# Retention in a two-layer trunk: queries transposed two heads at a time into the keys' PSUM bank, decayed halves made by four VectorE multiplies

## The chip, the cores and the metric

The kernel runs on one core of one Trainium2 chip. A core has five engines that run side by side, each through its own list of instructions in a fixed order: TensorE (PE, with its weight loads shown apart as PEld), VectorE (DVE), ScalarE (ACT), GpSimd (POOL) and SyncE (SP), which here issues the DMAs. They wait for each other on semaphores. The metric is device time in microseconds (us); lower is better.

## The reference, cut to what matters

The program is one inference step of a trunk of two layers with 1280 tokens (256 of new context and 1024 latent ones, which also read a cache of 512). Each layer makes an input projection, feeds three token mixers from it (retention, grouped-query attention, latent attention), multiplies their outputs by a gate and projects back. The change lies in retention alone, which works on chunks of 128 tokens, four heads of 64 channels:

```python
def step(s, inp):
    qi, ki, vi = inp
    a = jnp.einsum('bihd,bjhd->bhij', qi, ki) * intra
    o = (jnp.einsum('bhij,bjhe->bihe', a, vi)
         + jnp.einsum('bihd,bhde->bihe', qi, s) * q_dec[None, :, :, None])
    s = s * c_dec[None, :, None, None] + jnp.einsum('bjhd,bjhe->bhde', ki * k_dec[None, :, :, None], vi)
    return s, o
```

It is run forward and backward over the tokens, and the two outputs are added and normalized. The kernel does both directions at once: a head's 64 query channels stand twice on the 128 partitions, in the upper half times the forward decay and in the lower half times the backward one, against a state that is stacked in the same way.

## The kernel before

A layer begins with projections. The last of these is the gate (`z_blk`, L671 to L693): long runs of matmuls at L683, L684 and L685 (128x512 or 128x256 results, called z below), each result followed by a tanh on ACT (L688), a multiply on DVE (L690) and a store by SP (L691). After every block `z_blk` pulls once at a generator, `aside` (L709), which hands out the layer's other work piece by piece: rotated keys, latents, retention, and then the first tiles of attention (`att.prepare`). So retention's small matmuls stand between z's, and z covers the waits of retention. A list scheduler in the framework then fixes the final order on every engine; the code's order is only its input.

Retention (L788 to L933) has a backward loop over the ten chunks that accumulates states (L834 and the lines at L821 to L845) and then a forward loop of 13 rounds in which four stages of different chunks overlap: `stage_c` of chunk t-2, `stage_b` of t-1, `stage_a` of t and `stage_d` of t-3.

- `stage_a`: POOL has copied the chunk's queries into a doubled tile `qq` (L399; every head's 64 columns twice). TensorE transposes it in four steps into a PSUM bank `pt` (L868) and the keys in two steps into a second bank `pk` (L871). DVE multiplies `pt` by the decays in one instruction of 128x512 (L875, gives `qdT`). ACT copies the queries from `pt` into the block-diagonal `BD` (L877, L878), which has one buffer, and the keys into `kT` (L880). The state for the next chunk is advanced on POOL (L825, L826).
- `stage_b`: two matmuls of keys and queries (L893), then the decay mask on DVE (L895, `At`).
- `stage_c`: eight small matmuls (L903, L904) into the bank of pool `o`, which has one bank; ACT squares them (L905), DVE sums (L907), runs a Newton iteration of 13 tiny instructions for the reciprocal root (L150 to L160) and scales (L910, `oret`). Since there is one such bank, L903 of the next chunk waits for L910.
- `stage_d`: two transposes of `oret` (L916) into the free half of `pk`, and a copy on ACT into `yx` (L917).

PSUM has eight banks: five for pool `acc` (z, and the results called m), two for `tp`, one for `o`. The tiles `kd`, `qq` and `At` share three buffers.

Behind retention the first tiles of attention come: SP loads pieces of the keys (L1086, L1090) and, in 16 issues a layer, the rotated latent keys (L1144); ACT casts them (L196, L1147); the first score matmuls are at L1247 and L1248, the softmax exponential on ACT at L1270, transposes of its result at L1288. The buffers of these tiles lie where retention's tiles were.

Of the kernel before, what the change touches and what calls it, by code (L numbers as in the profile page):

```python
# [10 lines left out]
F32 = mybir.dt.float32  # L11
# [3 lines left out]
ALU = mybir.AluOpType  # L15
# [3 lines left out]
P = 128  # L19
D = 1024  # L20
NL = 8
NT = 10
# [59 lines left out]
def hybrid_trunk(tc, I, O):  # L82
# [3 lines left out]
    V, A, G, T = nc.vector, nc.scalar, nc.gpsimd, nc.tensor  # L86
    dma = nc.sync.dma_start
    pin = tc.keep_in_program_order
# [23 lines left out]
    ident = cst.tile([P, P], F32, name="ident")  # L112
    dma(ident, I["ident"])
    yxs = cst.tile([P, NT, D], F32, name="yx")
    yx = [yxs[:, t, :] for t in range(NT)]
# [18 lines left out]
    def bank(tag):  # L134
        if tag == "o":
            return pp.tile([P, 512], F32, name=tag, tag=tag, bufs=1)
        if tag == "m":
            tag = "tp"
        bufs = {"acc": NACC, "tp": 7 - NACC}[tag]
        return pp.tile([P, 512], F32, name=tag, tag=tag, bufs=bufs)  # L140
# [257 lines left out]
    def pool_copy(o, i):  # L398
        return G.tensor_scalar(o, i, 1.0, 1.0, op0=ALU.mult, op1=ALU.mult)  # L399
# [388 lines left out]
    def retention(l, rt, load, kv):  # L788
# [12 lines left out]
        def h4(ap):  # L801
            return ap.rearrange("p (h d) -> p h d", h=4)

        F, B = slice(0, 64), slice(64, 128)
# [8 lines left out]
        decT = rt.tile([P, 4, 128], F32, name="decT")  # L813
# [4 lines left out]
        def advanced(eng, d, nxt, cur, inc=None):  # L818

            if inc is not None:  # L820
                eng.tensor_tensor(h4(nxt), h4(cur), bc(cdec[d], d.start, d.stop), op=ALU.mult)  # L821
                eng.tensor_tensor(nxt, nxt, inc, op=ALU.add)
            else:
                st = rt.tile([P, 256], F32, name="cur", tag="cur", bufs=2)[d]
                pin(eng.tensor_tensor(h4(st), h4(cur), bc(cdec[d], d.start, d.stop), op=ALU.mult))  # L825
                eng.tensor_tensor(nxt, nxt, st, op=ALU.add)  # L826

        def increments(t, kv):
            kd = rt.tile([P, 4, 2, 64], F32, name="kd", tag="kd", bufs=3)
            V.tensor_tensor(kd, h4(kv[:, 0:256]).unsqueeze(2).to_broadcast([P, 4, 2, 64]),  # L830
                            dec[:, 2:4, :].rearrange("p a h -> p h a").unsqueeze(3).to_broadcast([P, 4, 2, 64]), op=ALU.mult)
            ps = bank("m")
            for h in range(4):
                T.matmul(ps[:, h * 64:(h + 1) * 64], kd[:, h, :, :].rearrange("p a b -> p (a b)"),  # L834
                         kv[:, 256 + h * 64:256 + (h + 1) * 64], start=True, stop=True)

            if t not in (0, NL, NT - 1):
                advanced(V, B, S[B, t - 1, :], S[B, t, :], ps[B, :256])
            elif t == NL:
                advanced(V, B, fin[B, :], S[B, t, :], ps[B, :256])  # L840
            elif t == NT - 1:
                V.tensor_copy(S[B, t - 1, :], ps[B, :256])

            if t != NL - 1:
                A.copy(S[F, t + 1, :] if t != NT - 1 else fin[F, :], ps[F, :256])  # L845

        qqs = {}

        def doubled(t):
            if t < NT:  # L850
                qqs[t] = rt.tile([P, 4, 2, 64], F32, name="qq", tag="kd", bufs=3)
                pin(pool_copy(qqs[t], h4(yx[t][:, 0:256]).unsqueeze(2).to_broadcast([P, 4, 2, 64])))

        for t in range(NT - 1, -1, -1):
            yield
            nx_kv = load(t - 1) if t else load(0)
            increments(t, kv)
            if t < 2:
                doubled(1 - t)
            kv = nx_kv  # L860

        BD = rt.tile([P, 2, 256], F32, name="BD")
        V.memset(BD, 0.0)

        def stage_a(t, kv, qq):
            pt = bank("tp")
            for h in range(4):
                T.transpose(pt[:, h * 128:(h + 1) * 128], qq[:, h, :, :].rearrange("p a b -> p (a b)"), ident)  # L868
            pk = bank("tp")
            for j in range(2):  # L870
                T.transpose(pk[:, j * 128:(j + 1) * 128], kv[:, j * 128:(j + 1) * 128], ident)  # L871
            if t >= 3:
                stage_d(t - 3, outs.pop(t - 3), pk[:, 256:512])
            qdT = rt.tile([P, 4, 128], F32, name="qdT", tag="qdT", bufs=2)
            V.tensor_tensor(qdT.rearrange("p h c -> p (h c)"), pt, decT.rearrange("p h c -> p (h c)"), op=ALU.mult)  # L875
            pq = pt.rearrange("p (j x c) -> p x j c", j=2, x=2)
            A.copy(BD[0:64, :, 0:128], pq[0:64, 0])  # L877
            A.copy(BD[64:128, :, 128:256], pq[64:128, 1])  # L878
            kT = rt.tile([P, 2, 128], F32, name="kT", tag="kT", bufs=1)
            A.copy(kT.rearrange("p j c -> p (j c)"), pk[:, 0:256])  # L880

            if t < NL - 1:
                advanced(G, F, S[F, t + 1, :], S[F, t, :])
            elif t == NL:
                advanced(G, F, fin[F, :], S[F, NT - 1, :])
                for d in range(2):
                    dma(new_state[0, l, d].rearrange("h d e -> d h e"), h4(fin[64 * d:64 * d + 64, :]))
            return kv, qdT, kT

        def stage_b(kT):  # L890
            pa = bank("m")
            for j in range(2):
                T.matmul(pa[:, j * 256:(j + 1) * 256], kT[:, j, :], BD[:, j, :], start=True, stop=True)  # L893
            At = rt.tile([P, 4, 128], F32, name="At", tag="kd", bufs=3)
            V.tensor_tensor(At.rearrange("p h c -> p (h c)"), pa, MT.rearrange("p h c -> p (h c)"), op=ALU.mult)  # L895
            return At

        def stage_c(t, kv, qdT, At):
            bo = bank("o")
            po, sq = bo[:, 0:256], bo[:, 256:512]  # L900
            for h in range(4):
                hs = slice(h * 64, (h + 1) * 64)
                T.matmul(po[:, hs], At[:, h, :], kv[:, 256 + h * 64:256 + (h + 1) * 64], start=True, stop=False)  # L903
                T.matmul(po[:, hs], qdT[:, h, :], S[:, t, hs], start=False, stop=True)  # L904
            A.activation(sq, po, AF.Square)  # L905
            ss = sm.tile([P, 4], F32, name="ss4", tag="ss4")
            V.tensor_reduce(ss, h4(sq), axis=AX.X, op=ALU.add)  # L907
            rstd = newton(ss, 4, 1.0 / 64)
            o = rt.tile([P, 256], F32, name="oret", tag="cur", bufs=2)
            V.tensor_tensor(h4(o), h4(po), bc(rstd), op=ALU.mult)  # L910
            return o

        def stage_d(t, o, pt):

            for i in range(2):
                T.transpose(pt[:, i * 128:(i + 1) * 128], o[:, i * 128:(i + 1) * 128], ident)  # L916
            A.copy(yx[t][:, 0:256], pt)  # L917

        st, At, outs = {}, {}, {}
        for t in range(NT + 3):  # L920
            yield
            if 2 <= t < NT + 2:
                outs[t - 2] = stage_c(t - 2, st[t - 2][0], st[t - 2][1], At.pop(t - 2))
            if 1 <= t <= NT:
                At[t - 1] = stage_b(st[t - 1][2])
            if t < NT:
                nx_kv = load(t + 1) if t + 1 < NT else None
                if t:
                    doubled(t + 1)
                st[t] = stage_a(t, kv, qqs.pop(t))  # L930
                kv = nx_kv
            elif t >= 3:
                stage_d(t - 3, outs.pop(t - 3), bank("tp")[:, :256])  # L933

    def cache_keys(l, pool, bufs):
# [565 lines left out]
    def open_p1(ws):  # L1501
        st = ExitStack()
        p1 = st.enter_context(tc.tile_pool(name="p1", reuse_waits="tile", bufs=1))
        ws.p1 = p1
        acts = [[p1.tile([P, KC, m * 128], F32R, name=f"a{x}{b}") for x in "hl"] for b, m in BLOCKS]
        return st, p1, acts
# [11 lines left out]
    st, p1, acts = open_p1(ws)  # L1518
# [66 lines left out]
    for l in range(DEPTH):  # L1585
        ws = Weights(out_blocks(l) + (in_blocks(l + 1) if l + 1 < DEPTH else []))
        att.run(ws)
        st, p1, acts = open_p1(ws)
# [104 lines left out]
```

## Time and profile before

| | us |
|---|---|
| median of three runs | 2163.22 (2162.13 to 2165.70) |
| the profiled execution | 2162.85 |
| its span in the trace | 2161.1 |
| PE busy in the span | 2084.2 (96%) |
| DVE / ACT / POOL busy | 1502.0 / 1183.5 / 978.2 |

The span is what the trace covers; 1.75 us of the profiled execution lie around it. Times in rows are counted from the start of the span. An item such as "[1.18 <-DVE oret L910]" behind a row says that the engine stood idle for 1.18 us before this instruction, and that DVE's write of `oret` at L910 ended the wait. Layer 0's retention loop lies at about 411 to 488 us, layer 1's at about 1454 to 1529 us.

### The profile page before, as it was taken

Reading aid. Unit: us, or ns where it says so; the run is one execution under the profiler, and the core shown is the slowest. Engines: PE = TensorE matmul, PEld = TensorE weight load, DVE = VectorE, ACT = ScalarE, POOL = GpSimd, SP = SyncE. Lnnn points to the kernel's source line nnn. Section 1 sums busy time; section 2 is a strip of 40 time slices with the busy share of each in tenths; the row PEclk is TensorE's granted clock in tenths of the full one; section 3 lists DMA queues with packets and bytes.
Section 4 is the critical chain, followed back from the end, with each engine's and each line's share of the span. In section 5 each row is a group of like instructions: output and inputs, shape, how many; then the busy total and the mean of one; then the engine's idle time right before and its main releaser. Section 6 shows DMA issues by size and latency. Waiting matters only on the chain. (4 is left out here: it accounts for less than half of the span.)

```text
span 2161.1 us, 42292 instructions
## 1 busy us (share of the span) xinstructions
PE 2084.2 (96%) x14888; PEld 1870.0 (87%) x14888; DVE 1502.0 (70%) x3830; ACT 1183.5 (55%) x3180; POOL 978.2 (45%) x1444
## 2 busy tenths in 40 slices
PE   7999999999999999999999999998999999999998
PEld 3899987788888888888999999887788888888898
DVE  4625583666889999997174358546689899999824
ACT  3503333225788888886243233322488888888623
POOL 2341242315576465533543324233375656453474
PEclk8999999999999999999999999999999999999999
DMA  9542446414111010004143212452311111000322
GB/s 315 145 145 63 123 112 204 122 49 117 36 44 28 20 30 25 13 27 136 46 153 102 66 54 55 140 152 66 109 46 30 32 30 32 14 22 18 98 91 98
DMA packets 189117, 173.30 MB, mean 80 GB/s; under 512 B 35833, under 2 KB 171625, under 8 KB 188905
## 3 DMA queue, kind: packets, MB, share of 16 engines
q1 hardware_dynamic: 187464, 165.35, 25.7%
q10 hardware_dynamic: 1440, 5.24, 0.6%
q8 instruction: 119, 1.95, 0.4%
q14 instruction: 94, 0.76, 0.1%
HBM read 124.77 MB, written 45.76 MB: 79 GB/s over the span
## 5 line engine op out<-in xcount | busy, mean ns | idle before, releaser
L256 PE MATMUL acc<-wh,ah 128*128 128x256 f32 (+1 forms) x1760 | 503.4, 286 | 1.8 <-ACT ah L404 1.8
L258 PE MATMUL acc<-wh,al 128*128 128x256 f32 (+1 forms) x1760 | 500.6, 284 | 2.5 <-DVE al L405 2.4
L257 PE MATMUL acc<-wl,ah 128*128 128x256 f32 (+1 forms) x1760 | 502.7, 286 | 0.0
L1256 DVE TENSOR_REDUCE nm<-acc 128x1 f32<-128x512 f32 (+1 forms) x624 | 411.7, 665 | 39.0 <-PE acc L1250 27.0
L1293 DVE TENSOR_TENSOR pT<-tp,pT 128x512 fp32r<-128x512 f32 (+1 forms) x624 | 413.2, 664 | 36.1 <-ACT pT L1292 30.6
L1292 ACT CAST pT<-tp 128x512 fp32r<-128x512 f32 (+1 forms) x624 | 356.5, 573 | 139.1 <-PE tp L1288 132.8
L1270 ACT ACTIVATE pn<-acc,nm 128x512 f32<-128x512 f32 (+1 forms) x624 | 421.3, 681 | 19.9 <-DVE nm L1261 17.4
L1288 PE MATMUL tp<-ident,pn 128*128 128x128 f32 x2400 | 424.1, 274 | 3.9 <-DVE pT L1293 2.4
L256 PEld LDWEIGHTS acc<-wh,ah 128*128 128x128 f32 x1760 | 334.9, 190 | 13.1 <-issue 8.2
L258 PEld LDWEIGHTS acc<-wh,al 128*128 128x128 f32 x1760 | 332.0, 189 | 5.3 <-DVE al L405 4.5
L257 PEld LDWEIGHTS acc<-wl,ah 128*128 128x128 f32 x1760 | 334.0, 190 | 0.8 <-issue 0.8
L1304 PE MATMUL o<-pT,V 128*128 128x256 f32 x1200 | 326.3, 294 | 0.7 <-DVE yx L1317 0.6
L1288 PEld LDWEIGHTS tp<-ident,pn 128*128 128x128 f32 x2400 | 287.6, 140 | 34.6 <-PE tp L1288 5.8
L1305 PE MATMUL o<-pT,V 128*128 128x256 f32 x1200 | 314.4, 284 | 0.0
L1304 PEld LDWEIGHTS o<-pT,V 128*128 128x128 f32 x1200 | 227.1, 189 | 19.2 <-DVE yx L1317 5.1
L1305 PEld LDWEIGHTS o<-pT,V 128*128 128x128 f32 x1200 | 227.2, 189 | 16.6
L192 POOL TENSOR_SCALAR wh<-raw 128x512 fp32r<-128x512 f32 (+2 forms) x144 | 82.4, 582 | 321.2 <-PE acc L258 143.2
L193 POOL TENSOR_TENSOR wl<-raw,wh 128x512 fp32r<-128x512 f32 (+2 forms) x144 | 164.7, 1155 | 5.2
L1247 PE MATMUL acc<-K,Qm 128*128 128x512 f32 (+1 forms) x312 | 140.6, 451 | 1.0
L683 PE MATMUL acc<-ah,wh 128*128 128x512 f32 (+1 forms) x384 | 141.4, 368 | 0.0
L684 PE MATMUL acc<-ah,wl 128*128 128x512 f32 (+1 forms) x384 | 139.8, 364 | 0.0
L685 PE MATMUL acc<-al,wh 128*128 128x512 f32 (+1 forms) x384 | 139.5, 363 | 0.0
(278 smaller groups left out, 3898.3 us busy)
## 6 DMA issues: line engine op xcount, KB each, us to landing
raw<-in_w_ada_dram SPq DMA_DIRECT2D x96, 256.0 KB, 3.2
raw<-in_w_in_dram SPq DMA_DIRECT2D x56, 256.0 KB, 2.9
kv<-s_rkv SPq DMA_DIRECT2D x40, 256.0 KB, 2.8
s_gT<-eo SPq DMA_DIRECT2D x80, 128.0 KB, 2.2
yx<-in_x_sample_dram SPq DMA_DIRECT2D x16, 512.0 KB, 6.4
gt<-s_gT SPq DMA_DIRECT2D x60, 128.0 KB, 2.1
raw<-in_w_in_dram SPq DMA_DIRECT2D x56, 128.0 KB, 2.5
raw<-in_w_out_dram SPq DMA_DIRECT2D x48, 128.0 KB, 3.0
```

Source lines behind the costliest of these rows:

```text
L193: G.tensor_tensor(wl, raw, wh.bitcast(F32), op=ALU.subtract)
L256: T.matmul(ps, ah[:, k, :], wh, start=(k == 0), stop=False)
L257: T.matmul(ps, ah[:, k, :], wl, start=False, stop=False)
L258: T.matmul(ps, al[:, k, :], wh, start=False, stop=(k == KC - 1))
L683: T.matmul(ps, wh, ah[:, k, :], start=(k == 0), stop=False)
L1256: V.tensor_reduce(nm[:, b:b + 1], ps, axis=AX.X, op=ALU.max, negate=True)
L1270: A.activation(pn, ps, AF.Exp, bias=p.ng[i], accum_out=p.su[:, i, b:b + 1])
L1288: T.transpose(pt[:, c * 128:(c + 1) * 128], pn[:, c * 128:(c + 1) * 128], ident)
L1292: A.copy(ph, p3)
L1293: V.tensor_tensor(pl, p3, ph.bitcast(F32), op=ALU.subtract)
L1304: T.matmul(p.po, vc, p.gran[b][:, 0, c, :], start=(ch == 0), stop=False)
L1305: T.matmul(p.po, vc, p.gran[b][:, 1, c, :], start=False, stop=(ch == last))
```

## The change

Queries are no longer doubled. `stage_a` transposes the queries as they are, two heads at a time, in two steps into the left half of one bank, and the keys in two steps into its right half. ACT's two copies into `BD` and the copy `kT` come first in the code; then DVE makes the decayed queries in four multiplies of 64 partitions and 2x128 columns, one for each direction and each head of a pair, so that two of them write to the other half of the partitions than they read. `stage_d` gets a bank of pool `tp` of its own in every round.

```diff
-        def doubled(t):
-            if t < NT:
-                qqs[t] = rt.tile([P, 4, 2, 64], F32, name="qq", tag="kd", bufs=3)
-                pin(pool_copy(qqs[t], h4(yx[t][:, 0:256]).unsqueeze(2).to_broadcast([P, 4, 2, 64])))
...
-        def stage_a(t, kv, qq):
+        def stage_a(t, kv):
             pt = bank("tp")
-            for h in range(4):
-                T.transpose(pt[:, h * 128:(h + 1) * 128], qq[:, h, :, :].rearrange("p a b -> p (a b)"), ident)
-            pk = bank("tp")
             for j in range(2):
-                T.transpose(pk[:, j * 128:(j + 1) * 128], kv[:, j * 128:(j + 1) * 128], ident)
-            if t >= 3:
-                stage_d(t - 3, outs.pop(t - 3), pk[:, 256:512])
+                T.transpose(pt[:, j * 128:(j + 1) * 128], yx[t][:, j * 128:(j + 1) * 128], ident)
+            for j in range(2):
+                T.transpose(pt[:, 256 + j * 128:256 + (j + 1) * 128], kv[:, j * 128:(j + 1) * 128], ident)
+            pq = pt[:, 0:256].rearrange("p (j c) -> p j c", j=2)
+            kT = rt.tile([P, 2, 128], F32, name="kT", tag="kT", bufs=1)
+            A.copy(BD[0:64, :, 0:128], pq[0:64])
+            A.copy(BD[64:128, :, 128:256], pq[64:128])
+            A.copy(kT.rearrange("p j c -> p (j c)"), pt[:, 256:512])
             qdT = rt.tile([P, 4, 128], F32, name="qdT", tag="qdT", bufs=2)
-            V.tensor_tensor(qdT.rearrange("p h c -> p (h c)"), pt, decT.rearrange("p h c -> p (h c)"), op=ALU.mult)
-            pq = pt.rearrange("p (j x c) -> p x j c", j=2, x=2)
-            A.copy(BD[0:64, :, 0:128], pq[0:64, 0])
-            A.copy(BD[64:128, :, 128:256], pq[64:128, 1])
-            kT = rt.tile([P, 2, 128], F32, name="kT", tag="kT", bufs=1)
-            A.copy(kT.rearrange("p j c -> p (j c)"), pk[:, 0:256])
+            for d in (F, B):
+                for x in range(2):
+                    q4, d4 = [a.rearrange("p (j x) c -> p x j c", x=2)[d, x] for a in (qdT, decT)]
+                    V.tensor_tensor(q4, pq[64 * x:64 * x + 64], d4, op=ALU.mult)
...
-            elif t >= 3:
+            if t >= 3:
                 stage_d(t - 3, outs.pop(t - 3), bank("tp")[:, :256])
```

The scheduler answers with another order in retention and in the first ten or so us of attention, alike in both layers; all else stays. Three places show it. Line numbers of the changed kernel are lower by 7 from `stage_b` on (L886 for L893, L896 for L903, L903 for L910, L909 for L916; in `stage_a` the transposes are L861 and L863, ACT's copies L866 to L868, the multiplies L873) and by 9 in attention (L1138 for L1147, L1261 for L1270).

First VectorE, one round of the loop in layer 0. Before, from one `oret` to the beginning of the next Newton iteration and its end:

```order
L910 TENSOR_TENSOR oret<-o,nwy 128x256
L895 TENSOR_TENSOR At<-tp,MT 128x512
L875 TENSOR_TENSOR qdT<-tp,decT 128x512
L907 TENSOR_REDUCE ss_5817<-o 128x4
L150 TENSOR_SCALAR nwx<-ss_5817 128x4
L151 TENSOR_SCALAR nwu<-nwx 128x4
L152 TENSOR_SCALAR nwy<-nwu 128x4
L153 TENSOR_SCALAR nwx<-nwx 128x4
L158 TENSOR_TENSOR nwu<-nwy 128x4
```

And of the changed kernel, a round in the same part of the loop:

```order
L903 TENSOR_TENSOR oret<-o,nwy 128x256
L873 TENSOR_TENSOR qdT<-tp,decT 64x2x128
L900 TENSOR_REDUCE ss_6043<-o 128x4
L873 TENSOR_TENSOR qdT<-tp,decT 64x2x128
L150 TENSOR_SCALAR nwx<-ss_6043 128x4
L873 TENSOR_TENSOR qdT<-tp,decT 64x2x128
L151 TENSOR_SCALAR nwu<-nwx 128x4
L873 TENSOR_TENSOR qdT<-tp,decT 64x2x128
L152 TENSOR_SCALAR nwy<-nwu 128x4
L153 TENSOR_SCALAR nwx<-nwx 128x4
L888 TENSOR_TENSOR At<-tp,MT 128x512
L158 TENSOR_TENSOR nwu<-nwy 128x4
```

The multiplies for the queries moved from ahead of the sum to between the instructions of the chain that ends in `oret`, three of the four behind the sum, and the mask's multiply `At` moved in there too.

Second TensorE in layer 0, from the end of one `stage_c` on. Before:

```order
L904 MATMUL o<-S,qdT 128x64
L893 MATMUL tp<-BD,kT 128x256
L868 MATMUL tp<-ident,qq 128x128 x4
L683 MATMUL acc<-ah_127,wh 128x512
L684 MATMUL acc<-ah_127,wl 128x512
L685 MATMUL acc<-al_128,wh 128x512
L683 MATMUL acc<-ah_127,wh 128x512
L871 MATMUL tp<-ident,kv 128x128 x2
L916 MATMUL tp<-ident,oret 128x128 x2
```

Changed, in the same part:

```order
L897 MATMUL o<-S,qdT 128x64
L909 MATMUL tp<-ident,oret 128x128 x2
L684 MATMUL acc<-ah_127,wl 128x512
L685 MATMUL acc<-al_128,wh 128x512
L683 MATMUL acc<-ah_127,wh 128x512
L886 MATMUL tp<-BD,kT 128x256 x2
L684 MATMUL acc<-ah_127,wl 128x512
L685 MATMUL acc<-al_128,wh 128x512
L683 MATMUL acc<-ah_127,wh 128x512
L861 MATMUL tp<-ident,yx 128x128 x2
L863 MATMUL tp<-ident,kv 128x128 x2
L684 MATMUL acc<-ah_127,wl 128x512
```

Four transposes of `qq` became two of `yx`, next to the keys', `stage_d` comes at once behind `stage_c`, and z matmuls stand between all stages. Over the whole loop, from the first transposes of queries to the last L916 (L909), the changed order has 149 z matmuls of 128x512 and 72 of 128x256, where before has 101 and 51; behind the last L916 it has 31 and 24 up to the first score matmul, where before has 67 and 24; ahead of the loop stand 12 of 128x512 and 21 of 128x256 fewer than before. Between two `stage_c` the changed order has 12 to 29 z matmuls of the two sizes (nine gaps: 12, 19, 16, 29, 15, 18, 19, 27, 15) where before has 8 to 24 (8, 12, 10, 11, 24, 12, 12, 12, 17).

Third ScalarE at the entry to attention in layer 0. Before:

```order
L688 ACTIVATE th<-acc 128x256
L1147 CAST kpr<-st 128x512
L688 ACTIVATE th<-acc 128x256
L1147 CAST kpr<-st 128x512 x2
L688 ACTIVATE th<-acc 128x256
L1147 CAST kpr<-st 128x256
L688 ACTIVATE th<-acc 128x256 x2
L1270 ACTIVATE pn,su<-acc,nm 128x512 x3
```

Changed:

```order
L688 ACTIVATE th<-acc 128x256 x2
L1138 CAST kpr<-st 128x512
L688 ACTIVATE th<-acc 128x256
L1138 CAST kpr<-st 128x512 x2
L1138 CAST kpr<-st 128x256
L1261 ACTIVATE pn,su<-acc,nm 128x512 x4
```

The tanhs of z moved ahead, since z ends sooner behind the loop; the first exponential stands behind the last cast of the rotated keys, as before.

## Rows read from the trace of the kernel before

**Rows 1.** The page: busy time of each engine, its share of the span, instructions.
```profile
PE 2084.2 (96%) x14888; PEld 1870.0 (87%) x14888; DVE 1502.0 (70%) x3830; ACT 1183.5 (55%) x3180; POOL 978.2 (45%) x1444
```

**Rows 2.** Windows: stretch, span, busy us of PE, PEld, DVE, ACT, POOL; granted clock; DMA.
```profile
411.00:489.00 78.00, 71.44 (x440) 61.49 (x440) 50.55 (x181) 21.47 (x62) 25.24 (x42) 0.96 0.22 62
1447.00:1530.00 83.00, 75.02 (x479) 64.11 (x478) 51.94 (x184) 22.15 (x64) 28.04 (x46) 1.00 0.22 61
...
441.00:444.00 3.00, 3.00 (x16) 2.61 (x16) 2.10 (x6) 1.64 (x5) 1.35 (x2) 0.64 0.30 87
...
484.00:488.00 4.00, 4.00 (x23) 3.74 (x23) 2.67 (x14) 0.38 (x1) 0.00 (x0) 0.72 0.01 2
```

**Rows 3.** Timeline of PE, layer 0's loop: start, duration, instruction, idle time before.
```profile
420.40 0.66 PE L868 MATMUL tp<-ident,qq 128*128 128x128 f32 x4 [1.30 <-POOL qq L399]
420.81 0.48 PE L685 MATMUL acc<-al,wh 128*128 128x512 f32 x1
...
473.26 1.02 PE L893 MATMUL tp<-BD,kT 128*128 128x256 f32 x4
474.12 0.42 PE L903 MATMUL o<-kv,At 128*128 128x64 f32 x2
...
478.50 0.39 PE L684 MATMUL acc<-ah,wl 128*128 128x512 f32 x1
...
478.95 0.28 PE L683 MATMUL acc<-ah,wh 128*128 128x256 f32 x1
479.07 0.28 PE L684 MATMUL acc<-ah,wl 128*128 128x256 f32 x1
...
480.90 0.41 PE L903 MATMUL o<-kv,At 128*128 128x64 f32 x2 [1.18 <-DVE oret L910]
...
482.49 0.39 PE L904 MATMUL o<-S,qdT 128*128 128x64 f32 x2
```

**Rows 4.** Tile view of the doubled queries, TensorE's group: ns as min/median/max.
```profile
L868 PE MATMUL tp<-ident,qq x80: 272/273/329, 411.5 to 1511.8; 128*128 128x128 f32 x80
```

**Rows 5.** Tile views of qdT and S: two VectorE multiplies that read PSUM, ns as above.
```profile
L875 DVE TENSOR_TENSOR qdT<-tp,decT x20: 681/688/692, 412.1 to 1512.6; 128x512 f32<-128x512 f32 x20
...
L822 DVE TENSOR_TENSOR S<-S,tp x14: 424/424/427, 384.1 to 1441.5; 64x256 f32<-64x256 f32 x14
```

**Rows 6.** Timeline of DVE, layer 0's loop: three chains from the sum to oret.
```profile
456.23 0.42 DVE L907 TENSOR_REDUCE ss<-o 128x4 f32<-128x256 f32 x1 [2.21 <-ACT o L905]
...
460.09 0.42 DVE L910 TENSOR_TENSOR oret<-o,nwy 128x256 f32<-128x256 f32 x1
...
477.05 0.65 DVE L150 TENSOR_SCALAR nwx<-ss 128x4 f32<-128x4 f32 x1
...
477.94 0.59 DVE L152 TENSOR_SCALAR nwy<-nwu 128x4 int32<-128x4 int32 x1
...
483.37 0.42 DVE L907 TENSOR_REDUCE ss<-o 128x4 f32<-128x256 f32 x1 [1.41 <-ACT o L905]
483.83 0.17 DVE L150 TENSOR_SCALAR nwx<-ss 128x4 f32<-128x4 f32 x1
...
486.21 0.42 DVE L910 TENSOR_TENSOR oret<-o,nwy 128x256 f32<-128x256 f32 x1
```

**Rows 7.** Timeline of SP at layer 0's entry to attention: start, time of the group's issues.
```profile
501.52 8.96 SPq L1144 DMA_DIRECT2D st<-s_kpT  x16
```

**Rows 8.** Timelines of PE and ACT at the same entry: start, duration, instruction, idle before.
```profile
487.87 0.38 PE L916 MATMUL tp<-ident,oret 128*128 128x128 f32 x2
...
513.97 0.40 ACT L1147 CAST kpr<-st 128x256 fp32r<-128x256 f32 x1
...
516.82 0.68 ACT L1270 ACTIVATE pn<-acc,nm 128x512 f32<-128x512 f32 x1
...
517.16 0.47 PE L1247 MATMUL acc<-K,Q 128*128 128x512 f32 x1 [0.71 <-DVE eo L690]
...
518.16 0.40 PE L1247 MATMUL acc<-K,Q 128*128 128x512 f32 x1
```

**Rows 9.** The line of the rotated keys' loads (L1144): issue to landing.
```profile
DMA to landing us min/median/max: 1.8/1.9/2.0
```

More of the change, by code (lines that the diff above doesn't have):

```diff
@@ L845, in increments @@
                 A.copy(S[F, t + 1, :] if t != NT - 1 else fin[F, :], ps[F, :256])
-        qqs = {}
-        def doubled(t):
-            if t < NT:
-                qqs[t] = rt.tile([P, 4, 2, 64], F32, name="qq", tag="kd", bufs=3)
-                pin(pool_copy(qqs[t], h4(yx[t][:, 0:256]).unsqueeze(2).to_broadcast([P, 4, 2, 64])))
         for t in range(NT - 1, -1, -1):
@@ L857, in retention @@
             increments(t, kv)
-            if t < 2:
-                doubled(1 - t)
             kv = nx_kv
@@ L927, in retention @@
                 nx_kv = load(t + 1) if t + 1 < NT else None
-                if t:
-                    doubled(t + 1)
-                st[t] = stage_a(t, kv, qqs.pop(t))
+                st[t] = stage_a(t, kv)
                 kv = nx_kv
-            elif t >= 3:
+            if t >= 3:
                 stage_d(t - 3, outs.pop(t - 3), bank("tp")[:, :256])
```

## The prediction

> **What bounds the kernel now.** The page first: TensorE is busy 2084.2 us of 2161.1, no other engine over 70% [rows 1]. A change pays only by taking instructions from PE or by closing its gaps. The windows come next, since the share says nothing of one stage: layer 0's retention loop, 411 to 489 us, has 78.00 - 71.44 = 6.56 us of PE idle, layer 1's, 1447 to 1530, has 83.00 - 75.02 = 7.98 [rows 2]. So 14.5 us is all that closed gaps in the loops can give. PE's timeline names them: 1.30 us once a layer in which the transposes wait for POOL's doubled queries, and mostly waits of L903 for `oret` of the chunk before, the last 1.18 [rows 3]. These come from a loop through three engines: end of L904, square on ACT, sum, Newton and scaling on DVE, next L903. PE fills it with z. Where the chain is longer than the work laid between two `stage_c`, PE stands.
>
> **TensorE's own work.** Four transposes a chunk become two. One lasts 273 ns by its row [rows 4], but four of them begin at 420.40 and the next matmul at 420.81 [rows 3]: 0.41 / 4 = 0.10 us of PE's time each, 0.11 with its neighbours. Twenty chunks in all lose two each: 40 x 0.11 = 4.4 us, 2.2 a layer. z is moved, not changed.
>
> **The copies on POOL.** They go, and with them the 1.30 us wait a layer (within the idle above). POOL's time is off the path elsewhere; I count nothing more.
>
> **VectorE's multiplies.** One of 128x512 takes 688 ns; the nearest row to the new ones is L822, which reads the same kind of bank over 64 partitions and 256 columns: 424 ns [rows 5]. Four are 4 x 0.424 = 1.70 us, 1.01 more than before, 10 us a layer more on an engine that has 27 of 78 us free there [rows 2]. What counts is where they stand: in the changed order one precedes the sum, hidden under ACT's square, and three lie inside the chain. [...]
>
> **The chain, after.** Without anything in between, sum to end of `oret` takes 486.21 + 0.42 - 483.37 = 3.26 us; with the mask and the one large multiply inside (and POOL's state update beside it) 460.09 + 0.42 - 456.23 = 4.28 [rows 6], that is 1.02 more for two instructions of 0.68. In the changed order the mask (0.68) and three multiplies of 0.42 are inside: 0.6 + 3 x 0.38 = 1.74 by start-to-start times of the same kind, so 5.0, and with 0.49 for the square (last L904's end, 482.49 + 0.39, to the sum at 483.37 [rows 3, 6]) and 0.06 for the release 5.6 us. Bounds: 5.2, if as much disappears into the gaps between tiny Newton instructions as above (4.28 + 0.34 + 0.55); 6.5, if instructions of the chain slow down as at 477.05 and 477.94, 0.65 and 0.59 where the same ones otherwise take 0.17 [rows 6], and a gate multiply of z falls in.
>
> **PE's work against it.** z matmuls start 0.23 us apart (512 columns: two in 478.95 - 478.50) and 0.12 (256); `stage_b` takes 474.12 - 473.26 = 0.86 [rows 3]. A gap of the changed order with 15 of 512: 3.5 + 0.86 + 4 transposes 0.45 + `stage_d` 0.22 = 5.0 us. In the same way the nine gaps come to 4.9, 6.2, 5.3, 5.6, 5.1, 5.8, 5.1, 5.6 and 3.8 (the last has neither mask nor queries: chain 4.0 to 4.8). Before they were 3.6 to 5.0 against some 4.8. So the loop has 13.7 us more z in it, which outweighs the longer chain: idle time s per layer is 0.7 + 0 + 0.3 + 0 + 0.5 + 0 + 0.5 + 0 + 0.6 = 2.6 at 5.6 us, with some 0.6 for loads of keys that SP issues later, s = 3.2. At a chain of 5.2, s = 1.2; at 6.5, s = 9.
>
> **Given back at the entry to attention.** The z that filled the loop is missing behind it: 36 matmuls of 512 columns, 36 x 0.23 = 8.4 us. What lies there is a chain on SP and ACT that begins when retention's tiles are free: the last L916 at 487.87, 16 loads of rotated keys from 501.52 for 8.96 us, 1.9 us to landing, a cast of 0.40, the first exponential of 0.68 [rows 7 to 9]. It can end no sooner than (501.52 + 8.96 + 1.9 + 0.40 + 0.68) - 487.87 = 25.6 us behind the last L916. Before, PE needed the exponential at 518.16 (the third score job of the second set), 30.3 us behind, so the chain was covered. Afterwards PE comes there after 30.3 - 0.7 (its wait for `eo`) - 8.4 = 21.2 us and waits 4.4. This is the new wait that the change brings, one per layer.
>
> **The sum.** Position of that score job against before: the last L916 comes later by the z (+8.4), earlier by the transposes (-2.2) and by the idle time closed (-(6.56 - s)); behind it 25.6 instead of 30.3 us. Layer 0: 8.4 - 2.2 - 6.56 + s + 25.6 - 30.3 = s - 5.1; layer 1, with 7.98: s - 6.5. At s = 3.2 that is -1.9 and -3.3, together **-5.2 us**: 2162.85 - 5.2 = 2157.65 for a profiled execution (1.75 around its span unchanged). That execution lay 0.37 below the median, so against 2163.22 I predict **2158.0**. Its own range follows from the chain: s = 1.2 gives -9.2, 2154; s = 5.5 (chain 6.0) gives -0.6, 2162.6.
>
> **Rivals.**
> - *Nothing is given back*: the loads of rotated keys start earlier than 13.65 us behind the last L916, since fewer gate stores stand between the issues on SP. Then the entry wait goes, and per layer only -2.2 - (6.56 - s) - 0.7 and -2.2 - (7.98 - s) - 0.7 remain, -6.3 and -7.7 at s = 3.2: 2149. For it: the issues are no longer held by z's stores. Against: the 16 loads alone take 8.96 us, and the casts ahead have their own loads. Chance 0.15.
> - *VectorE becomes the bound of the loop*: three multiplies inside the serial chain, with chain 6.5 and s = 9. Per layer 9 - 5.1 and 9 - 6.5: +6.4 us, 2169.6. The change loses from s = 5.8 on, a chain of about 6.1 us. For it: 4.28 with only two instructions inside, and the slow ones of 0.65 and 0.59; against: POOL, whose copies ran beside DVE, has less to do. Chance 0.22, a part of it within 0.2%.
> - *The clock decides*: in layer 0 PE's clock lay at 0.64 of 2.4 GHz at 441 to 444 us and at 0.72 at 484 to 488, PE busy all the time, the latter right behind the wait of 1.18 us; layer 1 had 1.00 in the same loop [rows 2, 3]. Without them PE saves 3 x 0.36 + 4 x 0.28 = 2.2 us; as many anew in layer 1 cost as much. On top of the forecast 2155.8 or 2160.2. The skill's page "TensorE: Matmul & The Clock Gate", section "Part 4: PE-mode transpose", has a rule for the first: transposes don't count as PE's activity for the clock gate; by it a loop with half the query transposes and more z keeps 2.4 GHz, for the former time. The trace speaks neither way, since layer 1 has as many transposes and no dip. Chance 0.08.
>
> **How the numbers follow.** The forecast has 0.55 (of which 0.30 below 2158.9, the rest within 0.2%), the entry's rival 0.15 (faster), VectorE's 0.22 (0.16 slower, 0.06 within), the clock's 0.08 (half and half). Within 0.2%, about 4.3 us, is what a measurement can't tell from no change: 2158.9 to 2167.5. Faster 0.30 + 0.15 + 0.04 = 0.49; same 0.25 + 0.06 + 0.04 = 0.35; slower 0.16. The range leaves out about 0.1 at either end: from half way into the entry's rival, 2148, to a chain of 6.4, 2169.
>
> **What would show it.** Right: L868's rows with 40 fewer matmuls; four multiplies of 0.42 a chunk; PE idle 2 to 4 us in each loop instead of 6.6 and 8.0, the waits of L903 for `oret` below 0.8 each; a new wait of 3 to 5 us of a score matmul for the first exponential, and ACT idle before it for a cast or its DMA. Wrong: sum to `oret` beyond 5.6 us and L903 waiting over 0.9 in most rounds (then slower); no wait at the first scores (then 2149); transposes or multiplies with other durations than their neighbours' rows.

## The result and the profile after

The changed kernel takes 2190.42 us (median, 2189.72 to 2192.71), the kernel before 2162.68 beside it: a ratio of 1.0127, interval 1.0110 to 1.0145, some 27.5 us slower, where 2158.0 was forecast. The page of the changed kernel, the lines that answer [rows 1]:

```profile
span 2187.9 us, 42175 instructions
...
PE 2094.3 (96%) x14848; PEld 1874.5 (86%) x14848; DVE 1526.3 (70%) x3890; ACT 1184.5 (54%) x3180; POOL 965.3 (44%) x1424
```

The span is 26.8 us longer. PE has 40 instructions fewer, as written, and yet is busy 10.1 us longer; the other 16.7 us are idle time (93.6 us instead of 76.9). So two things are to be found: what PE waits for, and why its work takes longer. The waits of PE in the changed kernel, summed by who is waited for (us in total, times, longest):

```profile
PE tp L1349 <- POOL rb L1346: 18.9, 6, 6.5
PE tp L861 <- DVE qdT L873: 10.7, 10, 3.8
PE acc L1238 <- ACT pn L1261: 5.6, 2, 3.3
...
PE o L896 <- DVE oret L903: 4.3, 14, 0.7
...
PE tp L909 <- DVE oret L903: 2.2, 2, 1.1
```

And the same view of the kernel before:

```profile
PE tp L1358 <- POOL rb L1355: 9.9, 6, 3.2
PE o L903 <- DVE oret L910: 9.3, 11, 1.2
...
PE tp L868 <- POOL qq L399: 2.3, 2, 1.3
...
PE acc L1247 <- ACT pn L1270: 1.3, 2, 0.7
```

Inside the loop the waits of `stage_c` for `oret` were halved (9.3 to 4.3 us), as forecast, but the last transposes now wait for it too (2.2), and the transposes of queries wait for the multiplies (10.7). Behind the loop two waits have grown: that for the first exponential (+4.3 us), which the prediction had, and one that it didn't name, for a small copy `rb` on POOL (+9.0). `rb` spreads the reciprocal softmax sums over 64 columns each; transposes bring it into place, some 76 us behind retention. Where these waits lie, on PE's timeline of the changed kernel:

```profile
420.81 0.66 PE L861 MATMUL tp<-ident,yx 128*128 128x128 f32 x2 [3.81 <-DVE qdT L873]
...
494.39 0.41 PE L909 MATMUL tp<-ident,oret 128*128 128x128 f32 x2 [1.08 <-DVE oret L903]
...
518.74 0.50 PE L1238 MATMUL acc<-K,Q 128*128 128x512 f32 x1 [2.33 <-ACT pn L1261]
...
570.40 0.69 PE L1349 MATMUL tp<-ident,rb 128*128 128x128 f32 x2 [6.52 <-POOL rb L1346]
...
1551.37 0.41 PE L909 MATMUL tp<-ident,oret 128*128 128x128 f32 x2 [1.08 <-DVE oret L903]
...
1627.74 0.69 PE L1349 MATMUL tp<-ident,rb 128*128 128x128 f32 x2 [5.81 <-POOL rb L1346]
```

Of the kernel before, the same places that front rows don't show:

```profile
564.80 0.69 PE L1358 MATMUL tp<-ident,rb 128*128 128x128 f32 x2 [2.22 <-POOL rb L1355]
...
1528.63 0.41 PE L916 MATMUL tp<-ident,oret 128*128 128x128 f32 x2 [0.29 <-DVE oret L910]
...
1604.67 0.44 PE L1358 MATMUL tp<-ident,rb 128*128 128x128 f32 x2 [1.29 <-POOL rb L1355]
```

Read in pairs: the last retention transposes lie at 487.87 before [rows 8] and 494.39 after, the first `rb` at 564.80 and 570.40. Between them 76.9 us before and 76.0 after; in layer 1, 76.0 and 76.4. Whatever the loop did, the first `rb` came some 76 us behind its end.

The longer busy time is mostly the clock. Windows of the changed kernel (span, busy us of PE, PEld, DVE, ACT, POOL, granted clock, DMA), around the first of layer 0's long waits and behind the one at the first `rb`:

```profile
418.00:420.00 2.00, 0.00 (x0) 0.00 (x0) 1.97 (x3) 0.00 (x0) 2.00 (x4) 1.00 0.35 96
...
422.00:424.00 2.00, 2.00 (x10) 2.00 (x11) 0.44 (x1) 0.00 (x0) 0.00 (x0) 0.50 0.13 41
424.00:426.00 2.00, 2.00 (x11) 2.00 (x11) 0.00 (x0) 0.34 (x1) 0.00 (x0) 0.50 0.00 0
426.00:428.00 2.00, 2.00 (x8) 1.68 (x8) 1.79 (x6) 1.41 (x5) 1.34 (x2) 0.66 0.42 131
...
571.00:573.00 2.00, 2.00 (x11) 2.00 (x11) 1.35 (x3) 0.00 (x0) 1.78 (x4) 0.50 0.07 20
573.00:575.00 2.00, 2.00 (x12) 1.73 (x11) 0.84 (x2) 1.53 (x4) 1.80 (x4) 0.72 0.00 0
```

PE stood still for 3.81 us, and right behind it, fully busy, it had 1.2 instead of 2.4 GHz for some 6 us. Call time multiplied by the missing share of the clock lost clock. Summed over 2 us windows, from the first z of a layer to 100 us behind its first `rb`, it is 11.9 us in each layer after, against 5.1 and 0.0 before. Some of it lies in idle time or in front of a wait that hides it. Within PE's busy time alone, over the whole trace, it is 13.3 us before and 25.3 after: 12.0 more, from which the transposes take back an estimated 4.4 (40 x 0.11). That leaves 7.6 of the 10.1 us of longer busy time; the other 2.5 stay open.

### The profile page after: what moved, and what is told of

It is laid out like the page before. It is cut to its first block, busy times and chain, and to the rows that moved or that the text cites. A ratio compares the mean times of both kernels' runs of the same rounds, so it can differ in the third digit from the quotient of the medians.

```text
span 2187.9 us, 42175 instructions
## 1 busy us (share of the span) xinstructions
PE 2094.3 (96%) x14848; PEld 1874.5 (86%) x14848; DVE 1526.3 (70%) x3890; ACT 1184.5 (54%) x3180; POOL 965.3 (44%) x1424
## 3 DMA queue, kind: packets, MB, share of 16 engines
q1 hardware_dynamic: 187464, 165.35, 25.3%
## 5 line engine op out<-in xcount | busy, mean ns | idle before, releaser
L1261 ACT ACTIVATE pn<-acc,nm 128x512 f32<-128x512 f32 (+1 forms) x624 | 421.0, 680 | 20.5 <-DVE nm L1252 17.8
L192 POOL TENSOR_SCALAR wh<-raw 128x512 fp32r<-128x512 f32 (+2 forms) x144 | 82.8, 585 | 326.9 <-PE acc L258 144.1
L193 POOL TENSOR_TENSOR wl<-raw,wh 128x512 fp32r<-128x512 f32 (+2 forms) x144 | 163.2, 1145 | 5.2
L1238 PE MATMUL acc<-K,Qm 128*128 128x512 f32 (+1 forms) x312 | 141.1, 452 | 1.0
L1239 PE MATMUL acc<-K,Qm 128*128 128x512 f32 (+1 forms) x312 | 139.5, 447 | 0.0
```

The costliest lines, as they stand in the source:

```text
L1238: T.matmul(ps, p.Q[:, 0, qs], K, start=True, stop=False)
L1239: T.matmul(ps, p.Q[:, 1, qs], K, start=False, stop=not p.mla)
L1261: A.activation(pn, ps, AF.Exp, bias=p.ng[i], accum_out=p.su[:, i, b:b + 1])
```

## The experiments

All are compared with the kernel before on the same chip, whose median was 2161 in each of these groups. The changed kernel has a group of its own (before 2162.68), so where an experiment is set against it, their distances from the kernel before are compared. The table holds what the traces of all gave, worked out from starts of rows, for layer 0 / layer 1: from the first transposes of queries to the last transposes of `oret` (the loop), from there to the first `rb`, and PE's wait there.

| kernel | median | loop | to first rb | wait at rb |
|---|---|---|---|---|
| before | 2162.68 | 76.4 / 74.8 | 76.9 / 76.0 | 2.2 / 1.3 |
| changed | 2190.42 | 91.7 / 92.0 | 76.0 / 76.4 | 6.5 / 5.8 |
| e1 split only | 2183.95 | 85.1 / 84.8 | 76.8 / 74.6 | 7.8 / 5.3 |
| e2 one multiply | 2167.85 | 82.2 / 82.2 | 76.9 / 76.5 | 2.3 / 1.4 |
| e3 later retention | 2173.01 | 78.5 / 78.4 | 76.4 / 75.8 | 4.0 / 3.6 |
| e4 own bank | 2162.68 | 75.8 / 75.8 | 76.2 / 77.8 | 1.7 / 2.8 |
| e5 before, rb on ACT | 2154.79 | 76.5 / 76.6 | 74.6 / 74.8 | 0 / 0 |
| e6 changed, rb on ACT | 2169.34 | 92.0 / 92.3 | 69.0 / 70.9 | 0 / 0 |
| e7 changed, no state on POOL | 2178.95 | 88.2 / 84.8 | 76.5 / 75.6 | 6.6 / 4.2 |
| e8 before, earlier | 2180.12 | 92.1 / 94.5 | 78.2 / 79.4 | 0.4 / 1.6 |
| e9 changed, pinned | 2169.03 | 83.3 / 83.6 | 76.3 / 77.5 | 0 / 2.0 |
| e10 e9 with rb on ACT | 2160.83 | 83.2 / 83.3 | 76.1 / 76.3 | 0 / 0 |
| e11 e10, splits moved | 2143.22 | 76.9 / 76.9 | 75.6 / 75.5 | 0 / 0 |
| e12 e5, splits moved | 2138.57 | 76.8 / 76.7 | 74.7 / 74.8 | 0 / 0 |

### Which part of the change costs: e1, e2, e4

e1 is the kernel before with the multiply split, and nothing else:

```diff
-            V.tensor_tensor(qdT.rearrange("p h c -> p (h c)"), pt, decT.rearrange("p h c -> p (h c)"), op=ALU.mult)
+            for d in (F, B):
+                for x in range(2):
+                    q4, p4, d4 = [... for a in (qdT, pt, decT)]      # 64 partitions x 2 x 128
+                    V.tensor_tensor(q4, p4, d4, op=ALU.mult)
```

> The kernel before, with the one multiply of 128x512 split into four of 64x256; doubled queries, both banks and ACT's copies stay. Theory M (three multiplies inside the serial chain lengthen it, the scheduler answers by laying 39 more z matmuls of 512 columns into the loop, so retention ends some 7 to 9 us later and with it all of attention's first tiles, and waits over 2 us drop the clock): 2175 to 2192. Rival B (the bank shared by queries and keys, in which ACT reads first, holds the transposes; the split itself is hidden): 2160 to 2168.

2183.95, ratio 1.0098 (1.0065 to 1.0130). Of 27.5 us, some 21 (14 to 28) come from the split alone, with the doubled queries and both banks in place. The loop grew by 9 to 10 us a layer, the wait at `rb` to 7.8 and 5.3. PE's idle time inside the loop did not grow: it is 6.6 and 6.2 us, where before has 6.5 and 7.5. The loop is longer by the 39 z matmuls of 512 columns that the scheduler laid into it (140 for 101, 39 x 0.23 = 9.0 us), and these are missing behind it.

e2 is the changed kernel with one multiply over the whole bank:

```diff
-            for d in (F, B):
-                for x in range(2):
-                    q4, d4 = [...]
-                    V.tensor_tensor(q4, pq[64 * x:64 * x + 64], d4, op=ALU.mult)
+            V.tensor_tensor(qdT.rearrange("p h c -> p (h c)"), pt, decT.rearrange("p h c -> p (h c)"), op=ALU.mult)
```

> The changed kernel with one multiply of 128x512 over the whole shared bank in place of the four (it takes the keys' half along, so the decayed queries are left out as such and the numbers differ). Theory M: 31 plus 60 z matmuls of 512 columns are again behind the loop as before the change, so 2152 to 2164, since 40 transposes and POOL's copies are saved. Rival B: the shared bank stays, so over 2175.

2167.85, ratio 1.0028 (1.0012 to 1.0044): some 21 us less than the changed kernel, at the same shared bank, but above the range that was expected. The loop still has 10.0 us of idle time a layer, 4.7 of them in one wait in the first round, for `oret`:

```profile
423.81 0.69 PE L893 MATMUL o<-kv,At 128*128 128x64 f32 x2 [4.69 <-DVE oret L900]
```

The first chain from sum to `oret` takes 9.2 us here, with one multiply in it, and 9.4 in the changed kernel. So it is not the split that stretches the first chain; e7 and e11 show what does.

e4 gives `stage_d` its own bank in the kernel before:

```diff
-            if t >= 3:
-                stage_d(t - 3, outs.pop(t - 3), pk[:, 256:512])
...
-            elif t >= 3:
+            if t >= 3:
                 stage_d(t - 3, outs.pop(t - 3), bank("tp")[:, :256])
```

> The kernel before, with a tp bank of its own for stage_d in every round, as the changed kernel has it; nothing else. Theory M: the order of z stays as before, at most some tenths per round of waiting for a bank: 2161 to 2167. Rival B (the banks): over 2172, since each transpose then waits for the multiply of the round before.

2162.68, ratio 1.0003 (0.9990 to 1.0016): nothing. Since e2 keeps the shared bank without the loss and e1 loses without a shared bank, the banks are not the cause.

### What the place of the loop costs: e3, e8

e3 starts retention two pulls later in the kernel before:

```diff
+                    for _ in range(2):
+                        yield
                     yield from retention(l, rt, load, kv)
```

> The kernel before, with retention started two pulls later, so that 26 fewer z matmuls of 512 columns lie behind the loop and it ends about 6 us later; no instruction of retention is changed. Theory D (attention's first loads wait for retention's end, and their chain through SP and POOL sets the first rb of attention): about 5 us later per layer at the first rb, with lost clock behind the longer waits 2170 to 2182. Rival E (only the length of the chain inside the loop costs): 2160 to 2166.

2173.01, ratio 1.0055 (1.0037 to 1.0073). No instruction was added, and the loop is only 2 to 4 us longer, but it ends 2.3 and 5.3 us later, counted from the layer's first z (some 6 were expected), and there is less z behind it: PE now waits for the first `rb` 4.0 and 3.6 us, at the same distance of 76 us:

```profile
488.46 0.44 PE L918 MATMUL tp<-ident,oret 128*128 128x128 f32 x2 [0.98 <-DVE oret L912]
...
564.86 0.69 PE L1360 MATMUL tp<-ident,rb 128*128 128x128 f32 x2 [4.04 <-POOL rb L1357]
```

The first `rb` comes 1.8 and 5.0 us later, 6.8 of the 12 us that e3 costs. Lost clock, summed as above, is 8.5 us in each layer, against 5.1 and 0.0 before; how the 12 us divide between the place of the loop and the clock this run can't tell.

e8 was to end it earlier (`LG = 24` for `LG = 6`):

> The kernel before, with the latents' work handed out in groups of 24 instead of 6 pieces per pull, so that retention starts some pulls earlier; 96 z matmuls of 512 columns are left behind the loop where before has 91. Theory D: the first rb of attention comes some 1 to 2 us earlier a layer, 2157 to 2161. Rival E (the place of the loop is indifferent): 2161 to 2166; if latents in one piece open waits of their own, later.

2180.12, ratio 1.0090 (1.0072 to 1.0108), a miss: the loop began 12.5 us earlier but took 92 instead of 76 us, with waits such as

```profile
430.25 1.11 PE L893 MATMUL tp<-BD,kT 128*128 128x256 f32 x3 [3.57 <-ACT kT L880]
```

so it ended later (491.0 for 487.9). It doesn't test an earlier end. What else its early loop ran into shows on VectorE in layer 1, beside GpSimd, which worked without a pause from 1472.52 to 1478.83:

```profile
1472.71 6.16 DVE L150 TENSOR_SCALAR nwx<-ss 128x4 f32<-128x4 f32 x1
```

In the first round of layer 0 the same instruction took 0.17 us. e7 and e11 take this up.

### The wait behind the loop: e5, e6

Both move the copy `rb` from POOL to ACT, in the kernel before and in the changed one:

```diff
-            G.tensor_scalar(rb..., ri.unsqueeze(2).to_broadcast([P, 4, 64]), 1.0, 1.0, op0=ALU.mult, op1=ALU.mult)
+            A.copy(rb..., ri.unsqueeze(2).to_broadcast([P, 4, 64]))
```

> The kernel before, with the small broadcast copy rb (128x256, the operand of the transposes at L1358) on ACT instead of POOL. Theory D (a queue on POOL that begins with retention's end holds the first rb, and PE waits for it, 9.9 us in six waits, with lost clock behind them): 2148 to 2158. Rival F (it is the data of attention that comes late, whichever engine copies): 2160 to 2167.

> The changed kernel with the same edit. Theory D: the waits of 6.5, 5.8 and twice 3.1 us and the half clock behind them go, so 12 to 22 us less than the changed kernel: 2168 to 2178; what is left over the kernel before with that edit is the longer loop alone, some 10 to 16 us. Rival F: 2186 to 2192.

2154.79 (0.9968, 0.9958 to 0.9978) and 2169.34 (1.0042, 1.0027 to 1.0057): 6 us less in the kernel before, some 19 less in the changed one, and in both the wait is gone. On ACT the copy starts 58 and 60 us behind the loop's end in e6, on POOL 76 in the changed kernel, so its operand is ready some 16 us before POOL comes to it. In e6 PE comes to the first `rb` 69 to 71 us behind the loop: so long PE's own work takes, since z is missing there, and 76 us are POOL's. In the kernel before PE's own work takes 74.7 (e5), just under POOL's. With `rb` on ACT in both, the change still costs 14.6 us. From a layer's first z to 100 us behind its first `rb` PE's idle time is 5.6 and 5.9 us longer in e6 than in e5, above all by the waits of the first round and at the exponential, and lost clock is 0 and 5.1 us more. Ahead of `rb` POOL prepares tiles of attention and makes a row of gate multiplies (L1335); the last four start 4.1 to 4.7 us apart for 1.3 us of work each:

```profile
554.72 1.29 POOL L1335 TENSOR_TENSOR yx<-yx,gr 128x512 f32<-128x512 f32 x1 [1.20 <-ACT pT L1283]
558.86 1.29 POOL L1335 TENSOR_TENSOR yx<-yx,gr 128x512 f32<-128x512 f32 x1 [2.85 <-DMA gr<-s_gT]
563.06 1.29 POOL L1335 TENSOR_TENSOR yx<-yx,gr 128x512 f32<-128x512 f32 x1 [2.91 <-PE o L1296]
...
567.79 1.26 POOL L1335 TENSOR_TENSOR yx<-yx,gr 128x512 f32<-128x512 f32 x1 [0.42 <-DMA gr<-s_gT]
...
569.94 0.41 POOL L1346 TENSOR_SCALAR rb<-ri 128x256 f32<-128x256 f32 x1
```

The profile puts two of these waits down to ACT and PE; in the kernel before the same three end with the load of `gr` (2.63, 2.84 and 2.85 us), which has one buffer, so the load is the likely cause of all. What ties the beginning of POOL's work to the end of the loop was not traced; that it keeps its distance is read from the table.

### Why the loop is long: e7, e9, e10, e11, e12

e7 leaves out the state update on POOL in the changed kernel:

```diff
-                advanced(G, F, S[F, t + 1, :], S[F, t, :])
+                pass
```

> The changed kernel without the forward state update on POOL in the loop (two POOL instructions of 0.6 and 0.7 us a chunk are left out, so the numbers differ); the order on the other engines is the same. Theory P (POOL's instructions stretch VectorE's tiny Newton instructions from 0.17 to over 1 us, and the transposes wait for the multiplies between them): the wait of 3.81 us shrinks below 2.5 and the loop gets 3 to 6 us shorter a layer, 2176 to 2186. Rival Q (VectorE's own work is the length, or POOL's weight splits alone): 2187 to 2192.

2178.95, ratio 1.0086 (1.0071 to 1.0101), 9 to 10 us less than the changed kernel. The first wait went from 3.81 to 1.98 in layer 0 and under 1 in layer 1, the idle time in the loops from 8.5 and 8.7 to 4.7 and 4.4. The rows of VectorE in the changed kernel's first round show what POOL did:

```profile
412.45 0.43 DVE L900 TENSOR_REDUCE ss<-o 128x4 f32<-128x256 f32 x1 [1.23 <-ACT o L898]
...
413.62 1.26 DVE L151 TENSOR_SCALAR nwu<-nwx 128x4 int32<-128x4 int32 x1
...
416.90 0.91 DVE L158 TENSOR_TENSOR nwu<-nwy 128x4 f32<-128x4 f32 x1
417.83 0.43 DVE L873 TENSOR_TENSOR qdT<-tp,decT 64x256 f32<-64x256 f32 x1
418.18 1.38 DVE L159 TENSOR_TENSOR nwu<-nwu,nwx 128x4 f32<-128x4 f32 x1
419.59 0.42 DVE L873 TENSOR_TENSOR qdT<-tp,decT 64x256 f32<-64x256 f32 x1
420.04 0.16 DVE L160 SCALAR_TENSOR_TENSOR nwy<-nwu,nwy 128x4 f32<-128x4 f32 x1
420.23 0.43 DVE L873 TENSOR_TENSOR qdT<-tp,decT 64x256 f32<-64x256 f32 x1
```

Beside them POOL, without a pause, state updates (L825, L826) and splits of gate weights (L192, L193):

```profile
416.01 0.61 POOL L825 TENSOR_TENSOR cur<-S,cdec 64x256 f32<-64x256 f32 x1
416.70 0.73 POOL L826 TENSOR_TENSOR S<-S,cur 64x256 f32<-64x256 f32 x1
417.40 0.77 POOL L192 TENSOR_SCALAR wh<-raw 128x256 fp32r<-128x256 f32 x2
418.14 1.40 POOL L193 TENSOR_TENSOR wl<-raw,wh 128x256 fp32r<-128x256 f32 x2
```

Instructions of 0.17 us take up to 1.38 us, and the fourth multiply, for which the transposes wait, stands behind them. In both kernels the splits run from 408.2 to 419.8 us. But retention starts 9 us earlier than before (402.7 for 411.4), so the first chain, which before began at 418.4 and met only the end of the splits (6.7 us), begins at 412.4 in their midst (9.4).

e9 keeps the instructions of the changed kernel and changes their order on VectorE: multiplies, mask and scaling are pinned to the code's order.

```diff
-                    V.tensor_tensor(q4, pq[64 * x:64 * x + 64], d4, op=ALU.mult)
+                    pin(V.tensor_tensor(q4, pq[64 * x:64 * x + 64], d4, op=ALU.mult))
```

(and in the same way for `At` and `oret`)

> The changed kernel with the same instructions, but the four multiplies, the mask and the scaling to oret kept in the code's order on VectorE, so that all four multiplies stand ahead of the sum and none inside the Newton chain; the scheduler then lays 126 z matmuls of 512 columns into the loop instead of 149 and 78 less 24 behind it instead of 55 less 24. Theory M (the multiplies' place in the chain, and through it the later end of retention): from retention's first transposes to its end some 6 to 8 us less a layer, 2166 to 2178. Rival S (four multiplies cost by being on VectorE at all, wherever they stand): 2184 to 2192.

2169.03, ratio 1.0039 (1.0025 to 1.0054): some 19 us less, by order alone. VectorE in one of its rounds:

```profile
459.56 0.68 DVE L888 TENSOR_TENSOR At<-tp,MT 128x512 f32<-128x512 f32 x1
460.16 1.72 DVE L873 TENSOR_TENSOR qdT<-tp,decT 64x256 f32<-64x256 f32 x4
462.96 0.42 DVE L900 TENSOR_REDUCE ss<-o 128x4 f32<-128x256 f32 x1 [1.07 <-ACT o L898]
466.01 0.42 DVE L903 TENSOR_TENSOR oret<-o,nwy 128x256 f32<-128x256 f32 x1
```

and in a round of the changed kernel:

```profile
476.22 0.42 DVE L900 TENSOR_REDUCE ss<-o 128x4 f32<-128x256 f32 x1
...
478.59 0.69 DVE L888 TENSOR_TENSOR At<-tp,MT 128x512 f32<-128x512 f32 x1
...
481.24 0.43 DVE L903 TENSOR_TENSOR oret<-o,nwy 128x256 f32<-128x256 f32 x1
```

From sum to the end of `oret` 3.47 us with the pins, 5.45 without; the mask and all four multiplies fit in front of the sum, with 1.07 us to spare. In such rounds they cost the chain nothing there. The loop is still 7 to 9 us longer than before, and the wait in the first round, now for `At`, is 5.8 us.

e10 adds `rb` on ACT:

> As e9, with rb's copy on ACT. Theory D: the waits behind retention's end go as well; 2152 to 2162, that is about the kernel before with rb on ACT (2155), less two transposes a chunk, plus a loop that is still some us longer. Rival S: 2166 to 2172, as the changed kernel with rb on ACT.

2160.83, ratio 0.9997 (0.9984 to 1.0010): the change, with the multiplies out of the chain and `rb` off POOL, is at par with the kernel before; but that one gains 6 us from the same edit of `rb` (e5). The first-round wait of 5.8 us was left. e11 and e12 take the splits of gate weights off POOL, e11 on top of e10, e12 on top of e5:

```diff
-                        split_w(raw[:, k, :n]...        # GpSimd both
+                        split_early(raw[:, k, :n]...    # ScalarE, VectorE
```

> As e10, with the weights' splits of 128x256 taken off POOL (the high part on ACT, the low part on VectorE). Theory P (POOL's weight splits beside the first round's Newton chain stretch its tiny instructions up to 1.7 us): the first chain falls from 9.0 us below 6, the wait of 5.8 us below 2.5, and with the half clock behind it 4 to 8 us a layer go: 2146 to 2154. Rival Q (VectorE gets the longer for it, nothing is gained): 2158 to 2168.

> The kernel before with rb on ACT and the same splits moved. Theory P: its first chain of 6.7 us shrinks too, but the wait there is only 1.3, so 0 to 6 us less than 2155: 2149 to 2155. If e11 lies below this one, two transposes fewer a chunk are worth their multiplies once the queues are cleared; if above, they aren't.

2143.22 (0.9914, 0.9900 to 0.9927) and 2138.57 (0.9896, 0.9883 to 0.9910), both below what was expected. In e11 the loop's idle time falls from 7.3 to 1.6 us a layer. The first chain, in the rows of e11's VectorE, takes 418.07 + 0.42 - 415.17 = 3.32 us, where the changed kernel needed 9.4:

```profile
415.17 0.42 DVE L900 TENSOR_REDUCE ss<-o 128x4 f32<-128x256 f32 x1
418.07 0.42 DVE L903 TENSOR_TENSOR oret<-o,nwy 128x256 f32<-128x256 f32 x1
```

Both beat both kernels. But e12, with the doubled queries, is the faster by 4.7 us. A likely cause, not tested: e11 has 23 z matmuls of 512 columns fewer behind the loop and waits there for `eo`, 3.89 us in layer 0 and 3.57 in layer 1, where e12 waits 0.7; lost clock is 5.1 us a layer in e11 and 0.0 in e12:

```profile
507.61 0.77 PE L1238 MATMUL acc<-K,Q 128*128 128x512 f32 x1 [3.89 <-DVE eo L690]
```

## Why the prediction was wrong

**What was right.** The 40 transposes and POOL's copies went, the multiplies took 422 ns each (median of 80), and 4 x 0.422 against 0.688, 1.00 us more, was the right price. The Trainium skill's page "Perfetto Trace Analysis", section "Optimizing Scalar/DVE Operations", puts the access overhead of a VectorE instruction at about 125 ns on PSUM, and advises larger operations where the engine is saturated. VectorE, at 70%, was not; and three instructions more would be an estimated 0.38 us by that figure, too little beside the measured 1.00. The chain from sum to `oret` had been put at 5.0 us, between 4.7 and 5.9; it measured 5.45 to 6.0 in the third to the eighth round. The steady waits were small: of 8.5 and 8.7 us of idle time in the loops, without the one wait of 3.8, some 4.8 are left, beside the forecast of 3.2. A new wait for the first exponential came, 2.3 and 3.3 us for 4.4.

**The step that failed: "Given back at the entry to attention".** It let the last transposes of `oret` come later and took 4.7 us back behind them, since the chain of loads, cast and exponential had 30.3 - 25.6 us of cover. For the first exponential that cover was there: in layer 0 the score job at which the sum ends came 1.2 us later than before, counted from the first z (199.3 for 198.1). But the sum ends there, 30 us behind the loop, as if nothing waited further on, and the prediction puts POOL at nothing without a row: "POOL's time is off the path elsewhere". The profile before already had PE waiting for `rb` on POOL, 2.22 and 1.29 us, 76 us behind the loop. With a wait at the end of a stretch of 76 us that moves with the loop, every us by which the loop ends later moves the first `rb` as well: in the sum, layer 0 is not s - 5.1 but 8.4 - 2.2 - 6.56 + s, and with the measured s = 8.5 that is +8.1 at the loop's end (measured: 175.0 for 167.8 us from the first z, +7.2). z that goes into the loop instead of behind it is then no gain but the price itself. e1 shows it with no new idle time in the loop, e6 by taking the wait away.

In layer 1 the same sum gives 8.4 - 2.2 - 7.98 + 8.7 = +6.9, and the loop ended 14.9 us later (177.7 for 162.8). Of the 8 us more, 5.1 are lost clock ahead of that end, where the trace before had none, and 1.8 idle time ahead of the loop; the rest is open.

**The size of s.** The rival that VectorE bounds the loop had s = 9 by longer chains in every round. s was 8.5 and 8.7, but 3.8 of it from one round: the first, because the transposes wait for the multiplies of the chunk before, and these stood between Newton instructions that POOL stretched. The prediction has no term for this wait; it counts those for `oret`, and it took POOL's lighter load for a help, where the earlier loop runs into POOL's weight splits. e7 and e11 show it. This rival gave 2169.6 and was nearest, but it lacked the place where the time is lost: e1 loses 21 us with no more idle time in the loop than before.

**The clock.** It was a rival of 2.2 us either way and was worth more. Each of the changed kernel's long waits from the loop on, 3.8 us in the loop, 2.3 to 3.3 at the exponential, 5.8 to 6.5 and twice 3.1 at `rb`, was followed by 3 to 7 us at 1.2 GHz, in both layers. But the length of a wait alone doesn't decide: the kernel before had waits of 3.19 and 2.92 us at a later `rb` of each layer without such a stretch; behind the waits of 1.07 and 1.18 us in its loops it had one each in layer 0 and none in layer 1, and the trace of e5, with the same loop, has them in both layers. So "waits over 2 us drop the clock", in the expectation of e1, is no rule that these traces bear out. The Trainium skill's page "TensorE: Matmul & The Clock Gate", section "Part 4: PE-mode transpose", has it that transposes don't count as activity; here fewer transposes and more z went with more lost clock, and the stretches at 1.2 GHz stand behind waits.

Nor does the clock need a change to move the time: the 22 executions of the kernel before beside e1 to e4 reach from 2155.38 us at a mean granted clock of 0.996 to 2169.82 at 0.990; those of the changed kernel had 0.982 to 0.985. How much of the 27.5 us is clock alone no run isolates, since waits and lost clock come together. In the two traces, as an estimate, the 26.8 us of longer span are 16.7 of idle time and 12.0 of lost clock in busy time, less 4.4 for the transposes, and 2.5 that stay open.

**The mechanism in one line.** Four multiplies, three of them inside a serial chain, make the scheduler lay z into the loop, which ends 7 to 15 us later; POOL's work up to the first `rb`, some 76 us behind that end, carries this to attention; lost clock behind the waits comes on top. About half of the loss is this path: with `rb` off POOL in both kernels, 27.5 us become 14.6, the waits of the first round and at the exponential and what clock goes with them. The part that was put at the centre, PE's instructions saved, is small: 4.4 us by the prediction's estimate, which no run measures by itself.

## What to carry to other kernels

Follow the work behind the edited stage until an engine shows a wait, not until the first number fits: a wait of 1 or 2 us far downstream can mean that the stage's end is already on the path, and filler that is drawn into the stage is then paid for. A multiply that is split in four is cheap or dear by its place: ahead of a serial chain of tiny instructions it cost the chain nothing (e9), inside it, with the mask, 2 us a round, and about 20 us in the whole by what the scheduler made of it. And ask what else runs beside the stage once it starts earlier; here GpSimd's splits were the collision, and moving them and one small copy gained 22 us in the kernel before, five times the 4.4 that the change was to save on PE.

## What the runs showed of the hardware

VectorE's Newton instructions on 128x4 elements took 0.15 to 0.17 us wherever no GpSimd instruction overlapped them (214 of 260 in the changed kernel), and up to 1.38 us beside GpSimd's elementwise work on SBUF, 1.71 in e9 and 6.16 in e8, where GpSimd ran that long without a pause. With GpSimd's splits moved, the first round's were back at 0.15 to 0.19 (e11, e12). The Trainium skill's page "Perfetto Trace Analysis", section "Optimizing Scalar/DVE Operations", says that the two engines share an SBUF read port; the traces agree with such a contention and add its size.

The new multiplies, two of which write to the other half of the partitions than they read, took 406 to 429 ns; those of e1, which all stay within their half, took 403 to 431.
